# Pacing the sums of weights in the up product with a copy of the newest split weights

## The chip, the cores and the metric

One core of a Trainium2 chip runs the whole kernel. The core has a matrix engine (TensorE, PE in the profile, with its weight loads as PEld), a vector engine (VectorE, DVE), an activation engine (ScalarE, ACT), a general engine (GpSimd, POOL) and a queue that mostly issues transfers (SyncE, SP). The metric is the device time of one execution in microseconds, the median of three runs: 2078.45 us before the change (2078.12 to 2079.34).

## The reference

One decoder block on 512 rows of 2048 channels, in float32. Cut to the part that the change touches:

```python
h = _rmsnorm(x, norm2_g[l])
up = jnp.einsum('bsd,df->bsf', h, ffn_w_up[l])        # 2048 -> 12288
up = _causal_dwconv(up, ffn_conv_w[l], ffn_conv_b[l]) # width 3
gate, val = jnp.split(up, 2, axis=-1)
x = x + jnp.einsum('bsf,fd->bsd', jax.nn.gelu(gate) * val, ffn_w_down[l])
return _rmsnorm(x, final_g)
```

Ahead of it stand an input projection, two token mixers (a gated one and a recurrent one) and an output projection, with the residual add.

## The kernel before

**Precision.** Each float32 operand is split into a high part h (a cast on ACT, line 126) and a low part l (the difference, on DVE, line 127); a product is three matmuls, h·h, h·l and l·h.

**Mixer stage** (to about 560 us). The input and output projections stream weights in chunks; they are not changed.

**Up and down products.** Both go by seven block products in place of eight: a tile of weights is seen as 2 x 2 blocks, and four sums of its blocks are needed beside three of the blocks themselves. The work is cut into units. A unit of the up product is one tile of weights (4 blocks of 128 x 256, 512 KB) against one tile of activations: 7 products x 2 halves x 3 matmuls = 42 matmuls of 128 x 256 (line 852). Eight units make a block of the output (`up_block`), and there are 24 blocks, 192 units: for each of 12 groups first the gate half, then the value half. A pair of blocks is 16 units.

A unit of weights goes through three steps (`Weights`, lines 628 to 652): `load` (SP, line 637, 512 KB into one of three `q` buffers), `sums` (three DVE adds, lines 646 to 648) and `pair` (the split into `wh` on ACT and `wl` on DVE, three buffers each). `prepare` runs these steps ahead: while unit u is multiplied, `pair` is done for unit u + 2, `sums` for the one behind it, and `load` for the one behind that. SP issues a load when the split that read the same `q` buffer has ended.

At the end of a block, `combine` (lines 865 to 876) adds the seven products from PSUM, one copy on ACT and seven operations on DVE. The convolution, the gelu and the product of gate and value of the block run spread over the first steps of the next one (`later`): in steps 1, 2, 4 and 5 DVE has a `rest` (line 916 twice, and in a value half line 919 too, behind which POOL stores the result with the transfer of line 921, `ad<-gate`).

**Sums of weights made by transfers.** For 54 units (eight at the start of the up product, the rest at its end and in the down product) DVE makes no sums. Their sums are put together in DRAM, in tiles `made`, by GpSimd transfers, of which all but the first two of a tile add to what is there: six transfers for each tile, 324 in all, mostly 256 KB each. The list is `to_make`, and `make` (line 315) issues the next n of it. In the mixer stage `make` is called with `after`, a column of the newest `wl`: GpSimd copies that column into `pace` (line 318) and so waits for the split. The mixer stage issues 144 of the 324, and 180 are left for the up product. There `make` is called once for each unit with the number that is due by then, without `after` (line 888). GpSimd takes its instructions in their written order; between the transfers of `make` it has the stores `ad<-gate`, which wait for DVE, and apart from these a transfer waits for the landing of the transfer that was issued eight before it on the same queue.

All engines run the up product in the order in which the code is written (`tc.manual_schedule`); DVE, ACT and SP have no other order to fall back on.

Of the kernel before, what the change touches and what calls it, by code (L numbers as in the profile page):

```python
# [8 lines left out]
F32 = mybir.dt.float32  # L9
# [69 lines left out]
def hybrid_block(ctx: ExitStack, tc: tile.TileContext, x, xT, w_in, w_out, w_up, w_dn, w_m4, w_dl, wab, wsT, vec, bs, vgb, fg, out):  # L79
# [5 lines left out]
    def psum(name, bufs):  # L85
        return tc.alloc_tile_pool(name=name, bufs=bufs, space=bass.MemoryType.PSUM, reuse_waits="tile")
# [34 lines left out]
    def col(at):  # L121
        return vc[:, at:at + 1]


    def split(h, l, src):
        nc.scalar.copy(h, src)  # L126
        nc.vector.tensor_tensor(l, src, h.bitcast(F32), ALU.subtract)  # L127
# [38 lines left out]
    def sl(pair, *idx):  # L166
        return tuple(t[idx] for t in pair)

    def cols(pair, i):
        return tuple(t[:, i * P:(i + 1) * P] for t in pair)  # L170
# [137 lines left out]
    to_make = []  # L308
# [6 lines left out]
    def make(n, after=None):  # L315

        if after is not None:
            nc.gpsimd.tensor_copy(pace, after)
        for _ in range(min(n, len(to_make))):
            add, dst, src = to_make.pop(0)  # L320
            how = {"accum_op": ALU.add} if add else {}
            nc.gpsimd.dma_start(dst, src, max_dma_last_dim=8192, **how)  # L322
# [305 lines left out]
    class Weights:  # L628
# [21 lines left out]
        def pair(self):  # L650
            self.hl = tuple(wq.tile([P, 7, 256], F32R, name=f"w{n}", tag=f"w{n}") for n in "hl")
            split(*self.hl, self.q[:, 0:7])

    act = {}

# [44 lines left out]
                split(*hl, self.q[:, 4 * i:4 * i + 4].rearrange("p a b -> p (a b)"))  # L700

    stream = []
    halves = []
    place, a_place = {}, {}
    done = [0, 0, 0]

    def rest_of_loads():
        while halves:
            halves.pop(0)()

    def prepare(upto, last=None):

        last = len(stream) - 1 if last is None else last
        for n in range(done[2], upto + 1):

            for i, step, ahead in ((0, "load", 1), (1, "sums", 1), (2, "pair", 0), (0, "load", 2)):
                for k in range(done[i], min(n + ahead, last) + 1):
                    if step == "sums":
                        rest_of_loads()
                    getattr(stream[k], step)()  # L720
                    done[i] = k + 1
# [7 lines left out]
    n_up = starts[0]  # L729
# [64 lines left out]
    def ready(u):  # L794

        if u < 7:
            return a_place[u + 1 if u else 0]
        n = len(units)
        return place[u + 3] - 1 if u + 3 < n else place[n - 1] + max(0, u - n + 2)
# [16 lines left out]
    n_make = len(to_make)  # L816
# [25 lines left out]
    def product(q, p, a, w, up, first, last):  # L842
        sa, sb = SLOTS[p]
        if first:
            q[p] = qbank().rearrange("p (t n) -> p t n", t=2)
        for t in range(2):
            s, r = ((w, sb), (a, sa)) if up else ((a, sa), (w, sb))
            sh, slo = (h[:, s[1], t * P:(t + 1) * P] for h in s[0])
            rh, rlo = (h[:, r[1]] for h in r[0])
            for n, (x_, y_) in enumerate(((sh, rh), (sh, rlo), (slo, rh))):  # L850

                nc.tensor.matmul(q[p][:, t], lhsT=x_, rhs=y_, start=first and t == 0 and n == 0, stop=last and t == 1 and n == 2, skip_group_check=True)  # L852
# [3 lines left out]
    def later(step, f):  # L856
        lazy.setdefault(step, []).append(f)

    def t_tile(name, shape, bufs=1):
        return pools["t"].tile(shape, F32, name=name, tag=name, bufs=bufs)  # L860
# [4 lines left out]
    def combine(q, c1, c11, c12, c21, c22):  # L865

        tt = nc.vector.tensor_tensor
        nc.scalar.copy(c1, q[1])  # L868
        tt(c11, c1, q[2], ALU.add)  # L869
        v, w = t_tile("v", [P, 2, 256]), t_tile("w", [P, 2, 256])  # L870
        tt(v, q[6], c1, ALU.subtract)
        tt(w, q[5], v, ALU.add)
        tt(c12, w, q[3], ALU.add)
        tt(c22, w, q[7], ALU.add)
        tt(v, v, q[7], ALU.add)
        tt(c21, q[4], v, ALU.subtract)
# [3 lines left out]
    def up_block(g, val, u0):  # L880
        q = {}
        for m in range(8):
            prepare(ready(u0 + m))
            for p in ORDER:
                product(q, p, act[m], stream[place[u0 + m]].hl, True, m == 0, m == 7)
                if p == 6:
                    rest_of_loads()
            make(len(to_make) - n_make + n_make * (u0 + m + 1) // (n_up - 16))
            if m == 7 and u0 == 0:
                pads[:] = [t_tile(f"pad{n}", [P, 2, S + 2]) for n in range(2)]  # L890
                for t in pads:
                    nc.gpsimd.memset(t[:, :, 0:2], 0.0)
            for f in lazy.pop(u0 + m, ()):
                f()
        c1 = t_tile("c1", [P, 2, 256])
        lo, hi = slice(2, 258), slice(258, 514)
        combine(q, c1, pads[0][:, :, lo], pads[1][:, :, lo], pads[0][:, :, hi], pads[1][:, :, hi])
        if u0 == 0:
            pools["ps"].release()
            pools["tr"].release()  # L900
            pools["ps"] = psum("q1", 8)

        def tap(n, j, f):
            if val:
                dst = t_tile("cv", [P, 2, S])if j == 0 else cvs[n]
                cvs[n] = dst
            else:
                if j == 0:
                    gates[n] = t_tile("gate", [P, 2, S], 2)
                dst = gates[n]  # L910
            nc.scalar.activation(dst[:, j], pads[n][:, j, 2:2 + S], AF.Identity, bias=col(V_FB + f), scale=col(V_FW + 2 * 96 + f))

        def rest(n, j, f):
            dst = (cvs if val else gates)[n][:, j]
            for i in (1, 0):
                nc.vector.scalar_tensor_tensor(dst, pads[n][:, j, i:i + S], col(V_FW + i * 96 + f), dst, ALU.mult, ALU.add)  # L916
            if val:
                gate = gates[n][:, j]
                nc.vector.tensor_tensor(gate, gate, dst, ALU.mult)  # L919
                at = 0 if j else 2  # L920
                nc.gpsimd.dma_start(ad[2 * g + n][:, at:at + 2], gate.rearrange("p (a b) -> p a b", a=2))  # L921

        def gelu(n, j):
            t = gates[n][:, j]
            nc.scalar.activation(t, t, AF.Gelu_apprx_tanh)

        cvs = {}
        at = u0 + 8
        for i, (n, j) in enumerate(((1, 0), (1, 1), (0, 0), (0, 1))):
            f = 48 * val + 4 * g + 2 * n + j  # L930
            step = at + (0, 1, 3, 4)[i]
            later(step, lambda n=n, j=j, f=f: tap(n, j, f))
            later(step + 1, lambda n=n, j=j, f=f: rest(n, j, f))
            if not val:
                later(step + 2, lambda n=n, j=j: gelu(n, j))

    pads = []
    for b, (g, val) in enumerate(ups):
        up_block(g, val, 8 * b)
# [181 lines left out]
```

## Time and profile before

| | |
|---|---|
| median of 3 runs | 2078.45 us |
| the profiled execution's own time | 2073.06 us |
| its span, first to last instruction | 2071.3 us |
| PE, DVE, ACT, POOL busy | 98%, 84%, 44%, 16% of the span |
| granted TensorE clock, mean | 0.995 |
| mixer stage / up product / down product (about) | 0 to 560, 560 to 1568, 1568 to 2071 us |

How to read it: a busy share is the share of the span in which at least one instruction of the engine was under way, and matmuls overlap, so a busy PE is not one at its peak; what a matmul costs in a dense stretch is the stretch divided by their number. "Waits" name the engine that waited and what ended its wait. The chain of waits is followed back from the last instruction; a transfer in it has the time from its issue to its landing. "To landing" of a group of transfers is counted from the issue too.

### The profile page before, as it was taken

To read this page: it belongs to the slowest core of one execution; us is meant where nothing else is said; L and a number is where in the kernel's file an instruction comes from. 1 tells how busy PE (TensorE), PEld (TensorE's weight loads), DVE (VectorE), ACT (ScalarE), POOL (GpSimd) and SP (SyncE) were. 2 spreads that over 40 slices of the span, in tenths; PEclk is the share of its full clock that TensorE was granted. 3 is DMA by queue.
4 is the path that set the end of the run, shared out by engine and by line. 5 is a ranking of instruction groups with operands and counts; after the bars stand their busy time and mean duration, and the time that the engine had idled before them with its cause. 6 is when DMAs were issued, how large, how long until landed. Compare 5 with 4: busy or idle time off the path is not lost.

```text
span 2071.3 us, 35056 instructions
## 1 busy us (share of the span) xinstructions
PE 2037.6 (98%) x14528; PEld 1921.8 (93%) x14528; DVE 1732.0 (84%) x2183; ACT 906.6 (44%) x887; POOL 323.7 (16%) x510
## 2 busy tenths in 40 slices
PE   9999999999989999999999999999999999999998
PEld 8888888888789999999999999999999999999996
DVE  7598982745379999999999999999989979879986
ACT  6445322423274444444444444444455345345443
POOL 1332232211210202202202012022000000000001
PEclk9999999999999999999999999999999999999999
DMA  7666687656553746647557467466456568558564
GB/s 250 181 171 163 175 213 175 192 170 213 148 156 112 199 127 177 180 131 193 148 151 203 136 173 191 136 175 168 128 205 221 189 216 284 181 192 282 176 231 153
DMA packets 105904, 376.37 MB, mean 182 GB/s; under 512 B 14608, under 2 KB 22160, under 8 KB 91792
## 3 DMA queue, kind: packets, MB, share of 16 engines
q1 hardware_dynamic: 65808, 246.30, 35.1%
q0 software_dynamic: 39360, 127.17, 25.9%
q8 instruction: 113, 1.85, 0.4%
q10 hardware_dynamic: 576, 0.66, 0.1%
q14 instruction: 47, 0.39, 0.1%
HBM read 341.57 MB, written 110.36 MB: 218 GB/s over the span
## 4 chain that ended last, share of the span: by engine, by line
PE 76%; DVE 17%; DMA 4%; issue 2%; ACT 1%; DVEq 0%; SPq 0%; ACTq 0%
PE qs L852 46%; PE ps L162 9%; PE ps L164 9%; PE ps L163 9%; DVE wl L127 7%; DMA q<-w_up 3%; DVE q L646 2%; DVE al L127 1%; DVE q L647 1%; DVE cv L916 1%; DMA q<-w_dn 1%; PE qs L163 1%; PE qs L162 1%; PE qs L164 1%; DVE gate L916 1%
## 5 line engine op out<-in xcount | busy, mean ns | idle before, releaser
L852 PE MATMUL qs<-ah,wh 128*128 128x256 f32 x2688 | 765.1, 285 | 6.4 <-DVE pad L869 3.9
L852 PE MATMUL qs<-al,wh 128*128 128x256 f32 x2688 | 762.5, 284 | 0.0
L852 PE MATMUL qs<-ah,wl 128*128 128x256 f32 x2688 | 762.3, 284 | 0.0
L126 ACT CAST wh<-q 128x1792 fp32r<-128x1792 f32 (+1 forms) x282 | 476.8, 1691 | 597.5 <-PE qs L852 382.9
L127 DVE TENSOR_TENSOR wl<-q,wh 128x1792 fp32r<-128x1792 f32 (+1 forms) x282 | 567.7, 2013 | 43.6 <-ACT wh L126 43.3
L852 PEld LDWEIGHTS qs<-ah,wh 128*128 128x128 f32 x2688 | 517.3, 192 | 9.3 <-DVE pad L869 5.1
L852 PEld LDWEIGHTS qs<-al,wh 128*128 128x128 f32 x2688 | 517.3, 192 | 0.1
L852 PEld LDWEIGHTS qs<-ah,wl 128*128 128x128 f32 x2688 | 517.3, 192 | 0.0
L852 PE MATMUL qs<-wh,ah 128*128 128x256 f32 x1232 | 351.0, 285 | 7.0 <-ACT c L868 3.4
L852 PE MATMUL qs<-wl,ah 128*128 128x256 f32 x1232 | 350.2, 284 | 0.0
L852 PE MATMUL qs<-wh,al 128*128 128x256 f32 x1232 | 350.1, 284 | 0.0
L852 PEld LDWEIGHTS qs<-wh,ah 128*128 128x128 f32 x1232 | 237.8, 193 | 8.5 <-ACT c L868 3.6
L322 POOL DMA_DIRECT2D made<-w_m x324 | 234.9, 1061 | 54.0 <-DMA made<-w_m 44.8
L127 DVE TENSOR_TENSOR wl<-wraw,wh 128x1024 fp32r<-128x1024 f32 (+2 forms) x105 | 118.0, 1127 | 149.4 <-ACT wh L126 144.5
L852 PEld LDWEIGHTS qs<-wl,ah 128*128 128x128 f32 x1232 | 237.9, 193 | 0.2 <-DVE wl L127 0.2
L852 PEld LDWEIGHTS qs<-wh,al 128*128 128x128 f32 x1232 | 237.8, 193 | 0.0
L126 ACT CAST wh<-wraw 128x1024 fp32r<-128x1024 f32 (+2 forms) x105 | 102.1, 974 | 273.4 <-PE ps L163 146.4
L646 DVE TENSOR_TENSOR q<-q 128x512 f32<-128x512 f32 x226 | 154.8, 685 | 22.1 <-DMA q<-w_up 18.6
L921 POOL DMA_DIRECT2D ad<-gate x48 | 28.0, 583 | 828.3 <-DVE gate L919 828.3
L162 PE MATMUL ps<-xgh,wh 128*128 128x512 f32 x384 | 152.5, 398 | 0.0
L163 PE MATMUL ps<-xgl,wh 128*128 128x512 f32 x384 | 152.2, 397 | 0.0
L164 PE MATMUL ps<-xgh,wl 128*128 128x512 f32 x384 | 150.2, 396 | 0.0
(242 smaller groups left out, 2491.5 us busy)
## 6 DMA issues: line engine op xcount, KB each, us to landing
q<-w_up SPq DMA_DIRECT2D x176, 512.0 KB, 3.6
made<-w_m POOLq DMA_DIRECT2D x270, 256.0 KB, 5.9
wraw<-w_in SPq DMA_DIRECT2D x28, 1024.0 KB, 6.3
q<-made SPq DMA_DIRECT2D x54, 512.0 KB, 4.0
q<-w_dn SPq DMA_DIRECT2D x50, 512.0 KB, 3.8
wraw<-w_out SPq DMA_DIRECT2D x16, 1024.0 KB, 5.5
q<-w_dn SPq DMA_DIRECT2D x38, 384.0 KB, 4.6
ad<-gate POOLq DMA_DIRECT2D x48, 256.0 KB, 2.4
```

The lines of the kernel that those rows point to most:

```text
L126: nc.scalar.copy(h, src)
L127: nc.vector.tensor_tensor(l, src, h.bitcast(F32), ALU.subtract)
L162: nc.tensor.matmul(ps, lhsT=ah, rhs=bh, start=start, stop=False)
L163: nc.tensor.matmul(ps, lhsT=ah, rhs=bl, start=False, stop=False)
L164: nc.tensor.matmul(ps, lhsT=al, rhs=bh, start=False, stop=stop)
L322: nc.gpsimd.dma_start(dst, src, max_dma_last_dim=8192, **how)
L646: nc.vector.tensor_tensor(q[:, 2:4], q[:, 5:7], q[:, 7:8].broadcast_to([P, 2, 256]), ALU.add)
L647: nc.vector.tensor_tensor(q[:, 1], q[:, 2], q[:, 6], ALU.add)
L852: nc.tensor.matmul(q[p][:, t], lhsT=x_, rhs=y_, start=first and t == 0 and n == 0, stop=last and t == 1 and n == 2, skip_group_check=True)
L916: nc.vector.scalar_tensor_tensor(dst, pads[n][:, j, i:i + S], col(V_FW + i * 96 + f), dst, ALU.mult, ALU.add)
L921: nc.gpsimd.dma_start(ad[2 * g + n][:, at:at + 2], gate.rearrange("p (a b) -> p a b", a=2))
```

## The change

Each split of weights (`Weights.pair`) leaves its `wl` in `latest`, and the up product hands `make` one column of it. So GpSimd copies that column ahead of the transfers of every unit, 192 copies more than before.

```diff
@@ -650,6 +650,7 @@
         def pair(self):
             self.hl = tuple(wq.tile([P, 7, 256], F32R, name=f"w{n}", tag=f"w{n}") for n in "hl")
             split(*self.hl, self.q[:, 0:7])
+            latest[:] = [self.hl[1]]
 
...
     stream = []
+    latest = []
     halves = []
...
-            make(len(to_make) - n_make + n_make * (u0 + m + 1) // (n_up - 16))
+            make(len(to_make) - n_make + n_make * (u0 + m + 1) // (n_up - 16), latest[0][:, 0, 0:1].bitcast(F32))
```

On GpSimd, in the middle of the up product, before (`made` are the tiles of sums, `w_m` the weights that they are made of, `ad` the stored result; a number behind a name tells tiles of one name apart):

```order
L921 DMA ad_3685<-gate 128x512
L322 DMA made_589<-w_m 32x2048 x2
L322 DMA made_588<-w_m 128x512
L322 DMA made_587<-w_m 128x256
L322 DMA made_591<-w_m 32x2048 x2
L322 DMA made_590<-w_m 32x2048 x2
L322 DMA made_589<-w_m 128x512
L322 DMA made_588<-w_m 128x256
L322 DMA made_592<-w_m 32x2048 x2
L921 DMA ad_3688<-gate 128x512
```

The same place on GpSimd after the change (lines are numbered two higher behind the added ones):

```order
L923 DMA ad_3685<-gate 128x512
L318 COPY pace<-wl 128x1
L322 DMA made_589<-w_m 32x2048
L318 COPY pace<-wl 128x1
L322 DMA made_589<-w_m 32x2048
L318 COPY pace<-wl 128x1
L322 DMA made_588<-w_m 128x512
L318 COPY pace<-wl 128x1
L322 DMA made_587<-w_m 128x256
L318 COPY pace<-wl 128x1
L322 DMA made_591<-w_m 32x2048
L318 COPY pace<-wl 128x1
```

The transfers keep their order, and a copy that reads a split stands ahead of each unit's one.

On DVE, in the middle of the up product, before, with what each instruction waits for (`wl` is the low part of the weights, `q` the buffer that they were loaded into):

```order
L648 TENSOR_TENSOR q<-q 128x256 [waits DVE_49]
L127 TENSOR_TENSOR wl<-q,wh 128x1792 [waits PE_49,Activation_49]
L916 SCALAR_TENSOR_TENSOR cv<-pad_4959,vc,cv 128x512
L916 SCALAR_TENSOR_TENSOR cv<-pad_4959,vc,cv 128x512 [waits DVE_49]
L919 TENSOR_TENSOR gate<-gate,cv 128x512 [waits DVE_49]
L646 TENSOR_TENSOR q<-q 128x512 [waits DMAHW5_49]
```

The same place on DVE after the change:

```order
L648 TENSOR_TENSOR q<-q 128x256 [waits DVE_49]
L127 TENSOR_TENSOR wl<-q,wh 128x1792 [waits PE_49,Activation_49,Pool_49]
L918 SCALAR_TENSOR_TENSOR cv<-pad_4967,vc,cv 128x512
L918 SCALAR_TENSOR_TENSOR cv<-pad_4967,vc,cv 128x512 [waits DVE_49]
L921 TENSOR_TENSOR gate<-gate,cv 128x512 [waits DVE_49]
L646 TENSOR_TENSOR q<-q 128x512 [waits DMAHW5_49]
```

The order on DVE is as it was; the split into `wl` now waits also for GpSimd, whose copy read the buffer's earlier content, three units back.

## Rows read from the trace of the kernel before

**Rows 1.** The page's part on busy time of each engine, its first line.

```profile
PE 2037.6 (98%) x14528; PEld 1921.8 (93%) x14528; DVE 1732.0 (84%) x2183; ACT 906.6 (44%) x887; POOL 323.7 (16%) x510
```

**Rows 2.** Busy time of each engine (and its instructions) in one stretch of the up product: from:to, length, PE, PEld, DVE, ACT, POOL, then the granted clock, the DMA engines' share and GB/s.

```profile
640.00:1560.00 920.00, 915.66 (x7604) 913.12 (x7604) 869.76 (x1090) 419.80 (x344) 143.97 (x206) 1.00 0.58 164
```

**Rows 3.** The chain of waits, one piece from the end of the up product: start, us, what.

```profile
1499.99 48.85 PE qs L852 x407
```

**Rows 4.** Waits of PE from 560 to 1600 us: us in total, times, longest.

```profile
PE qs L852 <- DVE pad L869: 4.5, 5, 1.7
PE qs L852 <- ACT c L868: 3.4, 1, 3.4
PE qs L852 <- DVE v L875: 2.4, 8, 0.3
```

**Rows 5.** Waits of DVE from 640 to 1500 us.

```profile
DVE q L646 <- DMA q<-w_up: 18.6, 19, 2.5
```

**Rows 6.** The chain of waits where DVE works without a break: start, us, what. First a combine, then two splits with a value half's rest between them, then three splits, the first two with a gate half's rest between them.

```profile
994.26 0.60 DVE pad L869
...
999.04 0.61 DVE q L646
...
1003.93 2.02 DVE wl L127
...
1009.56 2.02 DVE wl L127
...
1053.45 2.02 DVE wl L127
...
1058.36 2.02 DVE wl L127
...
1061.81 2.02 DVE wl L127
```

**Rows 7.** The chain of waits beside a train of made transfers.

```profile
1031.97 9.01 DMA q<-w_up
...
1041.00 0.70 DVE q L646
...
1044.58 7.32 DMA q<-w_up
...
1051.92 0.70 DVE q L646
```

**Rows 8.** Instructions of GpSimd in order of time: start, us, what, and in brackets the idle time before and what ended it.

```profile
1029.36 5.24 POOL L322 DMA_DIRECT2D made<-w_m  x7
1034.80 1.83 POOL L322 DMA_DIRECT2D made<-w_m  x3 [0.21 <-issue]
1037.04 0.79 POOL L322 DMA_DIRECT2D made<-w_m  x1 [0.40 <-DMA made<-w_m]
1038.10 0.78 POOL L322 DMA_DIRECT2D made<-w_m  x1 [0.28 <-DMA made<-w_m]
1041.90 0.81 POOL L322 DMA_DIRECT2D made<-w_m  x1 [3.03 <-DMA made<-w_m]
1091.27 0.61 POOL L921 DMA_DIRECT2D ad<-gate  x1 [48.55 <-DVE gate L919]
```

**Rows 9.** Loads of weights (line 637) in three stretches, each with its own count, first and last issue, and time to landing (least, median, most): 720 to 760 us, where GpSimd issues nothing; 677 to 704 us, where it issues single made transfers between stores, with the made transfers of 676 to 704 us themselves ahead of it; and 1029 to 1050 us, the train of rows 8.

```profile
L637 SPq DMA_DIRECT2D q<-w_up x8: 327/328/328, 721.7 to 757.2; - x8
...
DMA to landing us min/median/max: 3.4/3.5/4.0
...
L322 POOL DMA_DIRECT2D made<-w_m x7: 509/867/1135, 682.6 to 704.0; - x7
...
L637 SPq DMA_DIRECT2D q<-w_up x5: 327/328/328, 679.5 to 699.9; - x5
...
DMA to landing us min/median/max: 3.5/3.6/4.9
...
L637 SPq DMA_DIRECT2D q<-w_up x4: 328/328/328, 1032.0 to 1048.0; - x4
...
DMA to landing us min/median/max: 5.1/7.7/9.0
```

**Rows 10.** The copy that paces `make` in the mixer stage: on GpSimd with DVE idle behind the split, then beside DVE, and DVE's own operations at that time (two of line 370 in one row) and one of the same kind with no copy beside it.

```profile
310.60 0.18 POOL L318 COPY pace<-wl 128x1 f32<-128x1 f32 x1 [7.23 <-DVE wl L127]
311.04 2.98 POOL L322 DMA_DIRECT2D made<-w_m  x4 [0.25 <-issue]
...
66.06 0.57 POOL L318 COPY pace<-wl 128x1 f32<-128x1 f32 x1 [7.52 <-DVE wl L127]
...
65.84 1.41 DVE L370 SCALAR_TENSOR_TENSOR xr<-pad,vc,xr 128x512 f32<-128x512 f32 x2
67.77 0.75 DVE L370 SCALAR_TENSOR_TENSOR xr<-pad,vc,xr 128x512 f32<-128x512 f32 x1
```

**Rows 11.** The first units of the up product: GpSimd's train of made transfers, the chain of waits through a load that meets it, the activation ahead on ACT, and the wait of PE that follows.

```profile
586.45 6.00 POOL L322 DMA_DIRECT2D made<-w_m  x8
...
592.84 9.14 DMA q<-w_up
...
599.98 0.69 ACT L751 ACTIVATE q<-tr,vc 128x512 f32<-128x512 f32 x1 [0.75 <-PE tr L749]
...
606.65 0.66 PE L749 MATMUL tr<-ident,x 128*128 128x128 f32 x4 [1.24 <-ACT q L751]
```

## The prediction

> **What bounds the kernel now.** I read the page's busy shares first. PE is busy 98% of the span [rows 1], so only its idle time can be won, some 34 us in all, and the change touches only the up product. The windows show how much of that lies there. A dense stretch gives PE's own price: 48.85 us for 407 matmuls, 0.120 us each [rows 3]. From 640 to 1560 us there are 7604 matmuls, 912.5 us at that price, in 920.0 us [rows 2]. So the up product behind its first block loses 7.5 us on PE. The clock is 1.00 there, so the loss is waiting. PE's waits name who is waited for: DVE's combine, 4.5 us at line 869 and 2.4 us at line 875 [rows 4] (the matmuls' modelled tails hide some 0.15 us of every stall, so the list shows less than the count). The 3.4 us for the copy on ACT is one event behind the last block, where the loads of activations set the pace, and stays.
>
> Why is DVE late at some combines? Its own waits show one cause: 18.6 us, 19 times, for a load of weights [rows 5]. Now DVE's load without waits, from the chain [rows 6]. From split to split: 3.45 us with nothing between (1061.81 less 1058.36), 4.91 with a gate half's rest (1058.36 less 1053.45), 5.63 with a value half's (1009.56 less 1003.93); a combine is 4.78 us (999.04 less 994.26). A pair of blocks has 16 units, four rests of either kind and two combines: 16 x 3.45 + 4 x 1.46 + 4 x 2.18 + 2 x 4.78 = 79.3 us. PE needs 16 x 42 x 0.120 = 80.6 us for it. DVE has a margin of only 1.3 us for each pair. The waits are 18.6 us over 860 us, 1.76 us for each of 10.6 pairs: 81.1 us, more than PE's. So DVE with its waits sets the pace, and PE would without them; PE's loss of 7.5 us over 920 us (11.4 pairs) is 0.66 us a pair, close to 81.1 less 80.6.
>
> Where do the waits come from? In each pair GpSimd sits 48 us at a store that waits for DVE, and then issues all the made transfers that have become due, 13 in a train from 1029.36 on [rows 8]. A load of weights lands in 3.5 us with nothing beside it, in up to 4.9 us beside a store and one or two made transfers, and in up to 9.0 us in the train [rows 9]. Two loads of the train reach the chain of waits, 9.01 and 7.32 us [rows 7].
>
> **The change part by part.** *What it moves.* The 180 made transfers go out one for each unit (four units have two) over the first 176 units, in place of such trains. Number and bytes are the same. In a unit GpSimd copies the column when the split ends and issues behind it: in the mixer stage the transfer goes out 0.44 us behind the start of the copy [rows 10]. SP issues the next load at the end of the same split, so a load and one made transfer run side by side, in every unit.
>
> *What a load may take.* Between its issue and the adds that need it, DVE has the rest of its step, the next unit's adds and split (3.45 us), and the rest of that next step. The steps without a rest (0, 3, 6, 7) stand so that at least one rest or a combine always lies in the span, so the least is 4.91 us in a block with gate rests and 5.63 us in one with value rests [rows 6]. The landing with one made transfer beside it isn't in the trace as such: it lies between 3.5 us (nothing beside) and 9.0 us (the train). The nearest row is the stretch with seven made transfers and four stores, median 3.6 and at most 4.9 us [rows 9]; I take 4.2, below both limits. So DVE's 18.6 us of waits go, up to a rest of 2 us that the margin of 1.3 us a pair takes in. What is late next is PE itself: DVE then waits about 1.3 us a pair for it, at the splits or the combine. Gain: the 7.5 us.
>
> *The first units.* There GpSimd issues eight transfers within 6 us from 586.45 on [rows 11]. A load that meets them lands after 9.14 us, at 601.98; ACT was free at 600.67 (599.98 + 0.69), so 1.4 us are lost, of which PE shows 1.24 [rows 11]. With one transfer a unit this load takes about 5 us and is hidden by ACT's earlier work. Gain: 1.2 us.
>
> *What it adds.* 192 copies on GpSimd, 0.18 us each with DVE idle and 0.57 us beside DVE's operations [rows 10]: GpSimd has the time, being idle for 48 of some 81 us. DVE's pair of operations beside such a copy took 1.41 us and a single one without 0.75 us, so it is GpSimd that waits; I take 0 for DVE, and 0.39 us a copy as the other end. The split waits for the copy of three units back, some 15 us earlier. Behind a copy on GpSimd stand only that unit's transfer and the stores, and none of these is needed by an engine within a pair; behind the split on DVE stand the rests and the adds, and PE two units later, so a late copy would show there. I cost this wait at nothing; it would cost what GpSimd is late beyond 15 us, and its longest hold for a landing here is 3.03 us [rows 8].
>
> The Trainium skill (GPSIMD Engine Reference, section Specifications) says that GpSimd's access to SBUF is shared with VectorE and in contention with VectorE instructions that read two SBUF inputs, as the adds and the split here do. It does not say who waits: if GpSimd does, as the rows show, the copies cost nothing and the sum below stands; if VectorE does, the sum is that of the last rival.
>
> *The sum.* 7.5 + 1.2 = 8.7 us off the profiled execution's own 2073.06 us (span 2071.3 us). The median of the runs shown is 5.4 us above that execution; the stages are the same, so I take the gain off the median: 2078.45 - 8.7 = 2069.8 us.
>
> **The rivals.**
>
> *Half of it.* The trains go, but value-half steps, where a store and a made transfer run beside the load, and units with two transfers still make DVE late; the rests of combine (2.4 us at line 875 [rows 4]) and the start stay. Then about half, 4 us: 2074.5. For it: PE's waits are spread over several boundaries. Against it: the landing of at most 4.9 us where just this meets.
>
> *It moves the delay only.* One made transfer adds 1.6 us to each load (5.2 us landing): the five loads of a pair whose limit is 4.91 us come 0.3 us late each, 1.5 us a pair, what the trains cost now (1.76). 2078, no change. For it: the same bytes cross the same engines, and now always beside a load. Against it: at the pace of a single transfer the landing was 3.6 in the median.
>
> *Slower by contention.* From 5.1 us landing on, the loss passes the present one. At 5.5 us, about a third of the way from 3.5 to 9.0, the loads at 4.91 us come 0.6 us late, 3.0 us a pair: DVE then needs 82.3, which is 1.2 us a pair over the present 81.1, over 11.4 pairs 14 us: 2092.
>
> *Slower by the copies.* If DVE is the one that is held, 16 copies a pair at 0.39 us are 6.2 us: 79.3 + 6.2 = 85.5 us, 4.4 us a pair over now, 50 us: 2128. At 0.11 us a copy it would eat the gain. Against it speak DVE's two operations beside the copy [rows 10].
>
> **How the numbers follow.** The forecast has 0.63, half of it 0.14, no change 0.12, slower by contention 0.06, slower by the copies 0.05. A measurement tells about 0.2% (4.2 us) from no change. Faster takes the forecast and most of the half case (0.11 of 0.14): 0.74. No change takes its own 0.12 and the remaining 0.03: 0.15. Slower 0.11. The range: at the low end all of PE's 7.5 us, the 2.5 us more that a lag of DVE at the first boundary may give back (1.7 us is the longest wait there [rows 4]) and some spread of the runs, 2067.5; at the high end the case of no change, 2078.5. The slower cases and a little on the low side are left out. The forecast's own range is 2067.5 to 2073.
>
> **What would show it.** Right, step by step: GpSimd's row of trains becomes a copy and one transfer a unit, and its longest waits name the split; loads of weights land in about 4 us in the median and under 5.5 at most; DVE's 18.6 us of waiting for them fall under 3; PE's waits at lines 869 and 875 of before fall from 6.9 us to under 2; DVE begins to wait for ACT's cast or for PE's last product, about 1 us a pair; 640 to 1560 us hold some 60 matmuls more. Wrong: a median landing above 4.9 us, DVE's adds still waiting in most pairs, longer adds or splits on DVE (0.70 and 2.02 us now [rows 6, 7]), or a split that waits for GpSimd's copy.

## The result and the profile after

The changed kernel takes 2063.53 us (median of 4 runs, 2063.18 to 2065.96); the kernel before took 2078.28 us beside it (4 runs, 2074.13 to 2079.34). The ratio is 0.9939, with a 95% interval of 0.9927 to 0.9952 (the two medians alone give 0.9929): faster, by 10 to 15 us. Forecast were 8.7 us less, 2069.8 us, and a range whose low end was 2067.5. The direction and the mechanism were right, the gain was forecast too small.

The page's busy shares and the chain of waits, after (the first line answers to [rows 1]):

```profile
PE 2033.9 (99%) x14528; PEld 1920.2 (93%) x14528; DVE 1730.7 (84%) x2183; ACT 904.3 (44%) x887; POOL 418.7 (20%) x702
...
PE 93%; DVE 4%; DMA 1%; ACT 1%; issue 0%; SPq 0%; DVEq 0%; ACTq 0%
```

Before, the chain was 76% PE, 17% DVE and 4% DMA: DVE and the loads have almost left it. GpSimd's work has grown by 192 copies.

One stretch serves best to compare kernels, 640 to 1500 us: both multiply the up product there from end to end (the stretch to 1560 us of [rows 2] now takes in the passage to the down product, since that comes earlier). The windows of before, with 560 to 668 us, the first two blocks, ahead of it (columns as in [rows 2]; the two windows share 28 us):

```profile
560.00:668.00 108.00, 95.45 (x764) 92.98 (x763) 89.16 (x116) 60.75 (x59) 8.06 (x13) 0.97 0.44 133
640.00:1500.00 860.00, 855.66 (x7104) 853.12 (x7104) 816.84 (x1035) 387.99 (x319) 142.33 (x203) 1.00 0.58 162
```

The same windows after:

```profile
560.00:668.00 108.00, 96.58 (x769) 94.15 (x769) 89.61 (x117) 61.10 (x61) 21.38 (x30) 0.95 0.47 141
640.00:1500.00 860.00, 860.00 (x7169) 860.00 (x7168) 823.75 (x1045) 388.87 (x322) 223.47 (x384) 1.00 0.60 166
```

PE is busy 860 us of 860, with 7169 matmuls, and 860 us at 0.120 us [rows 3] hold 7167: the up product loses nothing in this stretch. Before, 65 matmuls were missing, 7.8 us. The chain of waits of after has one piece there where before had loads, adds and splits [rows 6, 7] (start, us, what), 0.120 us a matmul:

```profile
1099.99 200.04 PE qs L854 x1667
```

The waits after, of DVE from 640 to 1500 us [rows 5], then of PE from 560 to 1600 us [rows 4] (us in total, times, longest; lines are two higher):

```profile
DVE wl L127 <- ACT wh L126: 13.3, 11, 1.5
```

```profile
PE tr L751 <- ACT q L753: 9.2, 6, 3.4
PE qs L854 <- DVE pad L871: 2.4, 2, 1.8
PE qs L854 <- ACT c L870: 2.4, 1, 2.4
PE qs L854 <- DVE v L877: 0.3, 1, 0.3
```

DVE no longer waits for a load at all. It waits for ACT's cast instead, which is what an engine with time to spare does: the cast waits for PE to free a buffer (459.6 us in the whole run, by the page). Of PE's waits for DVE what is left lies at the first boundary and behind the last block; inside 640 to 1500 us there is none.

GpSimd after, in order of time, at the same place as [rows 8]:

```profile
1039.62 0.51 POOL L318 COPY pace<-wl 128x1 f32<-128x1 f32 x1 [6.47 <-DVE wl L127]
1040.07 0.51 POOL L322 DMA_DIRECT2D made<-w_m  x1
1043.07 0.57 POOL L318 COPY pace<-wl 128x1 f32<-128x1 f32 x1 [2.49 <-DVE wl L127]
1043.59 0.79 POOL L322 DMA_DIRECT2D made<-w_m  x1
1047.98 0.57 POOL L318 COPY pace<-wl 128x1 f32<-128x1 f32 x1 [3.60 <-DVE wl L127]
1048.49 0.78 POOL L322 DMA_DIRECT2D made<-w_m  x1
```

The train of 13 has become one copy and one transfer a unit. The loads of weights (line 637, 640 to 1490 us) in after:

```profile
L637 SPq DMA_DIRECT2D q<-w_up x168: 327/328/328, 644.4 to 1485.7; - x168
...
DMA to landing us min/median/max: 3.3/3.5/5.8
```

The median is that of a load with nothing beside it [rows 9]. Only the tail of the distribution has changed, as the same stretch of before shows:

```profile
DMA to landing us min/median/max: 3.3/3.6/9.9
```

### The profile page after: what moved, and what is told of

The parts are those of the page before. It is cut to its first block, busy times and chain, and to the rows that moved or that the text cites. A ratio compares the mean times of both kernels' runs of the same rounds, so it can differ in the third digit from the quotient of the medians.

```text
span 2061.6 us, 35459 instructions
## 1 busy us (share of the span) xinstructions
PE 2033.9 (99%) x14528; PEld 1920.2 (93%) x14528; DVE 1730.7 (84%) x2183; ACT 904.3 (44%) x887; POOL 418.7 (20%) x702
## 4 chain that ended last, share of the span: by engine, by line
PE 93%; DVE 4%; DMA 1%; ACT 1%; issue 0%; SPq 0%; DVEq 0%; ACTq 0%
PE qs L854 64%; PE ps L162 9%; PE ps L164 9%; PE ps L163 9%; DVE wl L127 1%; DMA q<-ad 1%; PE qs L163 1%; PE qs L164 1%; PE qs L162 1%; DVE al L127 1%; PE tr L751 0%; PE ps L582 0%; ACT wh L126 0%; DVE q L672 0%; DMA wraw<-w_in 0%
## 5 line engine op out<-in xcount | busy, mean ns | idle before, releaser
L126 ACT CAST wh<-q 128x1792 fp32r<-128x1792 f32 (+1 forms) x282 | 476.7, 1691 | 640.1 <-PE qs L854 459.6
L318 POOL COPY pace<-wl 128x1 f32<-128x1 f32 x236 | 125.8, 533 | 975.5 <-DVE wl L127 965.5
```

## Experiments

The interval of a ratio here is about 0.0013 to either side, 2.7 us; smaller terms can be told only in the traces.

**Again: the kernel before, twice more.** The changed kernel left two questions: was the profiled execution of before a typical one, and where does the rest of the gain come from? The first of these runs:

```diff
-    pace = const.tile([P, 1], F32, name="pace")
+    pace = const.tile([P, 1], F32, name="paced")
```

> The kernel before, with a tile renamed and nothing else. Theory A (the executions of the kernel before differ by what the trains of made transfers cost them, so that one profile may show a smaller loss than the median has): its times spread over several us, some 2073 to 2079, where the changed kernel's four lie within 2.8 us; and a profile's loss in the up product (920 us less 0.120 us a matmul, from 640 to 1560 us) goes with its time, 7.5 us at 2073 and about 12 us at 2078. Theory B (a fixed 5 us outside the up product that a profile doesn't show): all times lie close to 2078, the profile again some 5 us below them, the loss again 7.5 us.

It took 2077.36 us (12 runs, 2072.49 to 2079.02; ratio 1.0006, 0.9995 to 1.0017). The execution profiled took 2078.74 us, 5.7 us more than the profiled one of before. Later the same kernel was run once more, with another name for the tile:

> The kernel before once more, for the place of its spread: three profiles of it then stand beside the two of the changed kernel. Theory (the loss is variable and sits in the up product): the time falls anywhere from 2070 to 2083 us, DVE waits 18 to 26 us for loads of weights between 640 and 1500 us, and the window 640 to 1560 holds 7570 to 7605 matmuls; of what the execution has over the changed kernel's 2063.5 us, 8 to 12 us lie between 640 and 1560 and the rest, if any, before 640. Rival (the spread lies in the mixer stage or the down product, and the profiled execution's 7.5 us is the whole up loss in every execution): the window holds 7600 or more whatever the time.

2078.72 us. The windows of the first of these runs:

```profile
560.00:668.00 108.00, 93.87 (x723) 91.56 (x722) 86.40 (x113) 58.03 (x57) 7.86 (x13) 0.92 0.42 129
640.00:1500.00 860.00, 854.73 (x7088) 851.41 (x7088) 813.84 (x1031) 386.64 (x320) 141.74 (x202) 1.00 0.58 161
```

And of the second:

```profile
560.00:668.00 108.00, 95.43 (x746) 93.12 (x746) 87.42 (x115) 60.13 (x60) 8.06 (x13) 0.94 0.44 133
640.00:1500.00 860.00, 854.09 (x7077) 850.22 (x7076) 812.38 (x1028) 386.52 (x318) 141.74 (x202) 1.00 0.58 161
```

So executions near the median lose 81 and 92 matmuls from 640 to 1500 us, 9.7 and 11.0 us, and not 7.8 (Theory A named about 12 at 2078 us, Theory B 7.5 again). And from 560 to 668 us they have 41 and 18 fewer than the profiled one, 4.9 and 2.2 us; there the granted clock differs: 0.92 and 0.94 of full speed in place of 0.97. Over 108 us that is 5.4 and 3.2 us' worth of full clock, or 11 and 6 us more at the lower of the two levels (1.2 GHz). The stretch at half clock that all kernels show near 570 us, where PE waits 3.3 us for the activations, is longer, and there is more of it from 600 to 640 us (mean clock 0.91 and 0.96, against 1.00 in the profile of before). The loss is thus a variable one, in two places.

**The changed kernel again.**

> The changed kernel once more. Theory: 2063 to 2066 us, no wait of DVE for loads of weights from 640 to 1500 us beyond 1 us, 7640 to 7650 matmuls from 640 to 1560; the same start up to 632 us within 1 us as in its first profile. Rival (it too has executions that lose 5 us or more): a time of 2068 or above in this one or in one of its other runs.

2065.17 us (4 runs, 2064.03 to 2067.24; before beside it 2075.91, 9 runs; ratio 0.9944, 0.9929 to 0.9959). Its windows:

```profile
560.00:668.00 108.00, 96.15 (x751) 93.90 (x752) 88.08 (x116) 61.05 (x62) 21.19 (x29) 0.94 0.47 140
640.00:1500.00 860.00, 860.00 (x7169) 860.00 (x7168) 823.10 (x1044) 389.99 (x322) 223.92 (x384) 1.00 0.60 166
```

From 640 to 1500 us the loss is gone in both executions profiled: 7169 again. In the first two blocks the changed kernel varies too (751 and 769, with a mean clock from 600 to 640 us of 0.96 and 1.00), so "the same start within 1 us" was missed. The sum over the profiles: three of before hold 65, 81 and 92 matmuls less than 7169, 9.5 us in the mean; from 560 to 668 us before has 744 in the mean and the changed kernel 760, 1.9 us (nothing is counted twice: the 28 us that the windows share hold 233 or 234 in all five). Together 11.4 us; the mean spans, 2075.1 and 2063.55 us, differ by 11.5. The first term is the change's. The second, on so few executions of a varying stretch, can't be given to it.

**The two terms apart.** One kernel hands the column to the first block alone, the other to all but the first block:

```diff
# first_block
+            make(..., latest[0][:, 0, 0:1].bitcast(F32) if u0 == 0 else None)
# rest
+            make(..., latest[0][:, 0, 0:1].bitcast(F32) if u0 else None)
```

> The changed kernel with the pace in the first block (eight units) alone; behind it make has no copy, as before. By the terms of my sum: 1 us faster than before (the start), DVE's waits for loads from 640 to 1500 us still about 18 us. If the start is worth much more than a profile shows: 4 us and more faster.

> The changed kernel with the pace from the second block on alone: the first eight units' made transfers go out unpaced, as before. By the terms of my sum: within 1.5 us of the changed kernel's time, some 13 us faster than before, DVE's waits for loads under 1 us. If the start holds the missing 5 us: only 8 us faster.

The first block alone: 2075.73 us (12 runs, 2068.7 to 2077.28), ratio 0.9999 (0.9988 to 1.0009), no change; DVE still waits for loads, from 640 to 1500 us:

```profile
DVE q L646 <- DMA q<-w_up: 25.8, 22, 2.9
```

All but the first block: 2063.78 us (5 runs, 2063.06 to 2064.61), ratio 0.9946 (0.9932 to 0.9959), the whole gain within what can be measured. The windows, of the first block alone and then of all but the first block:

```profile
560.00:668.00 108.00, 96.75 (x763) 94.58 (x762) 88.40 (x115) 60.98 (x60) 20.01 (x25) 0.94 0.50 146
```

```profile
560.00:668.00 108.00, 96.40 (x764) 94.12 (x765) 89.39 (x117) 61.70 (x63) 9.16 (x17) 0.95 0.42 127
640.00:1500.00 860.00, 860.00 (x7169) 860.00 (x7168) 823.64 (x1046) 389.66 (x322) 224.26 (x384) 1.00 0.60 166
```

With the first block paced there are 763 matmuls from 560 to 668 us, without it 764. The forecast's term for the first units is not to be seen, neither in the time nor there; 1.2 us of time would be too little to tell.

**The copy without the wait.** If the copies themselves, and not the waiting, did it, a copy of a constant column would do it too:

```diff
-            make(len(to_make) - n_make + n_make * (u0 + m + 1) // (n_up - 16))
+            make(len(to_make) - n_make + n_make * (u0 + m + 1) // (n_up - 16), ones)
```

> The kernel before, with a copy of a constant column on GpSimd ahead of each unit's made transfers: the 192 copies without the wait for the split. If the spreading of the transfers is all that helps: trains as before, DVE waits for loads some 18 us, time as before (within 4 us of it). If the copies cost DVE something (0.11 us each and more): slower than before by 5 us and more. If the copies themselves break up the trains enough: faster by more than 4 us.

2081.25 us (7 runs, 2079.48 to 2083.55), ratio 1.0031 (1.0019 to 1.0043): slower than before. Its window from 640 us, and DVE's waits there:

```profile
640.00:1500.00 860.00, 848.78 (x7004) 843.42 (x7003) 804.37 (x1021) 382.07 (x315) 219.79 (x362) 1.00 0.57 160
```

```profile
DVE q L646 <- DMA q<-w_up: 30.3, 15, 7.3
```

165 matmuls are missing, 19.8 us. The expectation had put a slower time down to DVE being held by the copies. It isn't that: DVE's split and first add take 2018 and 684 ns in this stretch, as in the kernel before (2018 and 685), and its waits for loads have grown. GpSimd in a train of this kernel:

```profile
1362.31 0.84 POOL L322 DMA_DIRECT2D made<-w_m  x1
1362.86 1.89 POOL L318 COPY pace<-ones 128x1 f32<-128x1 f32 x1
1364.70 0.82 POOL L322 DMA_DIRECT2D made<-w_m  x1
...
1374.55 1.89 POOL L318 COPY pace<-ones 128x1 f32<-128x1 f32 x1
1376.38 0.78 POOL L322 DMA_DIRECT2D made<-w_m  x1
```

And its chain of waits there:

```profile
1372.26 0.69 DVE pad L876
...
1374.46 1.94 DVE wl L127
...
1376.42 12.13 DMA q<-w_up
```

The train is still there, since GpSimd still sits at the store and then makes up for it; with the copies between its twelve transfers it lasts 14.9 us (13 transfers took 13.4 us in [rows 8]), and the load issued at 1376.42, behind the combine, meets its end: 12.13 us. Why these trains cost more than those of before was not tried by itself. Of the wait this run is the proof: copies alone make it worse.

**Four at a time.** How short must a train be? Here `make` is called in every fourth unit, so one copy stands ahead of about four transfers:

```diff
+            if m % 4 == 3:
+                make(...)
```

> The changed kernel with make called in every fourth unit alone: one copy, then four made transfers. The same transfers, four trains of four a pair of blocks in place of 16 single ones (before: one train of some 13). If only long trains hurt: loads beside a train land in 4.5 to 6 us, DVE waits for loads 3 to 8 us in all from 640 to 1500 us, inside its margin of 1.3 us a pair, and the time is within 3 us of the changed kernel's 2063.5. If any clustering hurts: DVE waits 15 us and more, the time about 2072 to 2078.

2066.61 us (5 runs, 2064.43 to 2069.11; before beside it 2078.2, 15 runs), ratio 0.9949 (0.9936 to 0.9962). Landing of the loads, DVE's waits, and the window:

```profile
DMA to landing us min/median/max: 3.3/3.6/8.8
```

```profile
DVE q L646 <- DMA q<-w_up: 10.7, 10, 2.4
```

```profile
640.00:1500.00 860.00, 858.14 (x7145) 857.40 (x7144) 820.44 (x1041) 387.58 (x320) 163.35 (x256) 1.00 0.60 165
```

Trains of four still make a load late in one of some 17, more than expected (10.7 us of waits against 3 to 8, landings of up to 8.8 us against 6), but 10.7 us over 10.7 pairs (860 / 80.6) are 1.0 us a pair, below the margin of 1.3: only 24 matmuls are lost, 2.9 us.

**More transfers beside each load.** One or two more of 256 KB in each unit, to spare DRAM, in the changed kernel; nothing of the computation changes:

```diff
+            for k in range(1 * (u0 + m), 1 * (u0 + m + 1)):
+                nc.gpsimd.dma_start(spare[0:32], w_m4[...], max_dma_last_dim=8192)
```

> The changed kernel with one transfer of 256 KB more in each unit, from the weights to a spare place in DRAM (extra work, the result is the same). If single transfers are hidden with room to spare: the median landing goes from 3.5 to about 4.2 us, DVE's waits for loads stay under its margin of 1.3 us a pair (15 us in all), the time within 3 us of the changed kernel. If the changed kernel was near the edge of contention: landings above 4.9 us in the median and 10 us and more slower.

> As the double one, with two transfers of 256 KB more in each unit. By the limits of 4.9 and 5.6 us: landings of about 5 us in the median, so that the five loads of a pair with the limit of 4.9 us come up to 1 us late: DVE waits 20 to 50 us from 640 to 1500 us, and the time is 5 to 35 us above the changed kernel's. If the limits don't matter: within 3 us of it.

With one more: 2069.98 us (5 runs, 2067.08 to 2071.31), ratio 0.9961 (0.9949 to 0.9974). With two more: 2079.15 us (11 runs, 2074.1 to 2082.82), ratio 1.0005 (0.9993 to 1.0016). Landings, and what DVE waited for, with one more:

```profile
DMA to landing us min/median/max: 3.4/3.9/7.1
```

```profile
DVE wl L127 <- ACT wh L126: 11.8, 11, 1.5
DVE q L646 <- DMA q<-w_up: 1.1, 2, 0.9
```

With two more:

```profile
DMA to landing us min/median/max: 3.4/5.1/8.3
```

```profile
DVE q L646 <- DMA q<-w_up: 13.5, 24, 1.3
DVE wl L127 <- ACT wh L126: 0.9, 2, 0.6
```

That agrees with limits of 4.91 and 5.63 us, and the change stays below them: it takes three transfers a unit to bring the median to 5.1, and even then the window from 640 us holds 7144 matmuls, a loss of 3.0 us, since the margin swallows most. DVE's 13.5 us are fewer than the 20 to 50 expected. With one transfer more the window holds 7169, no loss at all, and yet the time is 6.5 us above the changed kernel's, where at most 3 were expected. So what these two kernels lose besides lies outside this window. Part of it comes ahead of every added transfer: PE begins the up product at 567.5 and 567.6 us, in the two profiles of the changed kernel at 564.6 and 565.1. Why was not found out, so their times say little about the landings; the window does.

**DVE's margin, from both sides.** One of the three adds is repeated, with the same result, in every second unit and in every eighth:

```diff
             nc.vector.tensor_tensor(q[:, 1], q[:, 2], q[:, 6], ALU.add)
+            summed.append(0)
+            if len(summed) % 2 == 0:
+                nc.vector.tensor_tensor(q[:, 1], q[:, 2], q[:, 6], ALU.add)
```

> The changed kernel with one of the three adds of every second unit done twice (0.46 us each, the same result): 8 x 0.46 = 3.7 us more for DVE in a pair of blocks. By my sum (DVE 79.3 us, PE 80.6 us a pair): DVE becomes the bound by 2.4 us a pair, over 11.4 pairs 27 us slower than the changed kernel, about 2090. If DVE has more room than I worked out: within 10 us of it. If it sits on the path already: 42 us slower.

> The changed kernel with one of the three adds repeated in every eighth unit: two of them a pair of blocks, 2 x 0.46 = 0.92 us of DVE a pair, below the margin of 1.3 us. Theory (PE bounds the pair, and DVE has 1.3 us to spare): within 2 us of the changed kernel, 2063 to 2066; DVE's wait for ACT's cast falls by some 8 to 10 us from 13.3. Rival (DVE, not PE, sets the pace of the changed kernel's pair): 0.92 x 11.4 = 10.5 us slower, 2074.

Every second unit: 2089.5 us (4 runs, 2088.68 to 2091.32), ratio 1.006 (1.0045 to 1.0076). Every eighth: 2063.27 us (5 runs, 2062.64 to 2065.7), ratio 0.9939 (0.9927 to 0.9952). PE's waits with the add in every second unit, 640 to 1500 us:

```profile
PE qs L858 <- DVE pad L875: 14.9, 10, 1.7
PE qs L858 <- DVE v L881: 3.1, 10, 0.3
```

and DVE's waits there with the add in every eighth:

```profile
DVE wl L127 <- ACT wh L126: 4.3, 10, 1.5
```

0.92 us more of DVE a pair cost nothing, and come out of the 13.3 us for which DVE waited (9.0 of them). 3.7 us a pair cost 192 matmuls (6977 in the window), 23.0 us over 10.7 pairs, 2.2 us a pair: the margin is 1.5 us, beside the 1.3 of the forecast.

## Why the prediction was right in its mechanism and wrong in its size

**What bounds the kernel.** Right. PE's 0.120 us a matmul, DVE's margin of 1.3 us a pair and the trains as what eats it all hold: the margin by the two runs on DVE, the trains by the run with four at a time and by the one that copies without waiting.

**What a load may take.** The landing of 4.2 us was on the safe side (3.5 measured); its longest, 5.8, is over the 5.5 that I named as the most, and no wait came of it. The rival by which the change moves the delay only (5.2 us for each load), and contention (5.5), fall with that: two transfers more would be needed for the former's landing. The half case falls as well: no wait for a load is left to make DVE late.

**The first units.** The step happened: the load that met the train landed after 9.1 us and now after 6.0 (from its line's own view, issue at 593.7), and PE's wait of 1.24 us behind it [rows 11] is not there any more. But it earns nothing that can be measured, since this stretch varies by more from execution to execution (723 to 764 matmuls in before, 751 and 769 in the changed kernel). The 1.2 us should not have been added as if they were sure.

**What it adds.** Right, 0. The copies now wait and stretch on GpSimd, and DVE's operations keep their time, as the groups of after from 640 to 1500 us show (count, busy us, mean ns, idle before):

```profile
L127 DVE TENSOR_TENSOR wl<-q,wh 128x1792 fp32r<-128x1792 f32 x171 | 345.1, 2018 | 13.4 <-ACT wh L126 13.3
L646 DVE TENSOR_TENSOR q<-q 128x512 f32<-128x512 f32 x171 | 116.9, 684 | 0.0
```

The same view of before gives 2018 and 685 ns. So the rival that DVE is held by the copies falls, and the Trainium skill's rule (GPSIMD Engine Reference, section Specifications) on shared access to SBUF beside DVE's two-input instructions is met in the form that the rows spoke for: GpSimd is the one that waits. No split waited for GpSimd's copy.

**The sum.** Its step that failed is this one: "The median of the runs shown is 5.4 us above that execution; the stages are the same, so I take the gain off the median". It treats the 5.4 us as a constant that the change leaves alone, and takes a loss read from one execution as the loss of them all. The two later executions of before lie 5.7 us above the profiled one, and 1.9 and 3.2 us of that are more of the trains' loss (81 and 92 matmuls in place of 65). So the term for the up product, 7.5 us, was right for the one execution that it was read from (7.8 measured in the window to 1500 us) and too small for those near the median: 9.7 and 11.0 us, 9.5 in the mean of three. The other part, 4.9 and 2.2 us, lies in the first two blocks and goes with the granted clock; the changed kernel has such executions too, so it isn't shown to be the change's.

Against its own execution the sum was fair: 2073.06 less 2063.26 is 9.8 us, and 8.7 were forecast. Taken off the median it is short by 2.5 to 4 us of the 11.2 to 12.7 us that the ratios 0.9946 to 0.9939 give, and by 6 of the 14.8 us between the medians of the first runs. From the profiled execution itself the forecast would have been 2064.4 us, close to the 2063.5 measured, but in part by luck: that sum has the 1.2 us of the start in it, which no run shows in the time.

The low end of the range added to this. It reached down from 2069.8 and so took the shift over, and the 2.5 us that it gave to DVE's lag at the first boundary did not come: PE waits 1.8 us there now, 1.7 before.

Two slips of arithmetic change nothing: 601.98 less 600.67 is 1.3 us, not 1.4, and by the prediction's own figures the loss passes the present one from landings of 5.26 us on (five loads late by 0.35 us each), not from 5.1.

The spread of the runs points the same way without any trace: before's runs lie between 2070 and 2083 us, those of the changed kernel (this version, all but the first block, and the eighth add) between 2062.6 and 2067.2. A loss that varies from execution to execution takes some of the spread with it when it goes; that it takes all of the difference isn't shown.

**What would show it.** Of the signs named, there came: a copy and a transfer a unit; DVE's waits for loads under 3 us (none); DVE waiting for the cast, 13.3 us over 10.7 pairs, 1.2 us a pair, where about 1 was named; 65 matmuls more where 60 were named (in the window to 1500 us). PE's waits for DVE fell from 6.9 to 2.7 us, not under 2: the 1.8 us at the first boundary stayed.

## What to carry to other kernels

Where an engine has a margin of 1.3 us in 80, look at the longest landing of its loads and not at the median: a background stream that sits behind a wait comes out as a train, and pacing it by the consumer's own progress costs one tiny instruction a unit. The copy has to be a wait for that progress; a mere filler between the transfers made it worse here. Whether taking the waiting store off GpSimd's queue would do as well was not tried. And size a variable loss from several executions, or take the gain off the execution in which it was measured.

## What the runs showed of the hardware

The copy of one column on GpSimd can last until what DVE does beside it has ended. With DVE idle it took 0.18 us [rows 10]; beside the split of the activations in the first units of the changed kernel it took 1.84 us:

```profile
591.54 1.84 POOL L318 COPY pace<-wl 128x1 f32<-128x1 f32 x1 [30.56 <-DVE wl L127]
```

The split beside it, on DVE:

```profile
591.32 2.02 DVE L127 TENSOR_TENSOR al<-q,ah 128x1792 fp32r<-128x1792 f32 x1
```

Both end within 0.04 us of each other (593.38 and 593.34), and the split has its usual 2.02 us. In the kernel with the copies of a constant the longest copy was 2.79 us.

It depends on what DVE reads. Of the 171 copies from 640 to 1500 us, 21 took 0.18 us although DVE was at work, all of them beside the first sum of a combine, which has one of its two inputs (`qs`) in PSUM; the others ran beside the adds (64) or the rests (86), whose tensors all lie in SBUF, and all but one of them took 0.5 to 0.6 us. One of the 21, and what DVE does beside it:

```profile
1031.38 0.18 POOL L318 COPY pace<-wl 128x1 f32<-128x1 f32 x1 [2.16 <-DVE wl L127]
```

```profile
1031.17 0.68 DVE L871 TENSOR_TENSOR pad<-c,qs 128x512 f32<-128x512 f32 x1
```

A single transfer of 256 KB a unit costs a load of 512 KB nothing in the median (3.5 us with none and with one), two a unit cost 0.4 us and three 1.6. In a train of 13 the loads of before landed after 5.1 to 9.0 us [rows 9], though the bytes of a pair are those of one transfer a unit.
